# A hybrid decoder layer on one core: shift sums, load order, solve pace and short attention steps

## The chip, the cores and the metric

The kernel runs on one core of a Trainium2 chip. The core has a matrix engine (TensorE, PE in the profile, with its weight loads shown as PEld), a vector engine (VectorE, DVE), a scalar engine (ScalarE, ACT), a general engine (GpSimd, POOL) and a sync engine (SyncE, SP) that here issues nearly all DMA transfers. Each engine works off its own list of instructions in order; semaphores tie the lists together. The metric is the device time of one execution in microseconds (us), less is better.

## The reference

One decoder layer over 512 tokens of width 2048, in float32. Cut to its lines:

```python
mod = silu(c) @ w_ada + b_ada                       # c: [1, 2048], w_ada: [2048, 6144]
shift, scale, gate = split(mod, 3)
h = rms_norm(x, norm_w) * (1 + scale) + shift       # [512, 2048]
aq, ak, av, ag, d_qkv, dz, db, da, mg_a, mg_b = split(h @ w_in)
y_a = (window_attention(rope(norm(aq)), rope(norm(ak)), av, sinks) * silu(ag)) @ w_o_swa
q, k, v = split(silu(causal_conv(d_qkv)))           # 16 + 16 + 32 heads of 128
o = gated_delta_rule(norm(q), norm(k), v, g(da), beta(db))   # chunks of 64, a triangular inverse in each
y_b = (rms_norm(o) * silu(dz)) @ w_o_dn             # w_o_dn: [4096, 2048]
y = sigmoid(mg_a) * y_a + sigmoid(mg_b) * y_b
return x + gate * (y @ w_out)
```

`shift` and `scale` are the two thirds of a vector-matrix product with a 2048 x 4096 weight matrix. The triangular inverse in each chunk is `inv(I + L)` with L strictly lower triangular.

## The kernel before

**Tiles.** All data stand with channels on the 128 partitions and the 512 tokens along the free axis. A float32 product is made of three matmuls on rounded halves: weights and inputs are split into a high part (ACT, `whi`, `hh`) and the remaining low part (DVE, `wlo`, `hl`), and `mm3` (L240 to 245) adds hi x hi, hi x lo and lo x hi into one PSUM tile. A `channel_tile` (L247) makes 128 output channels: 16 steps over the input channels (kt), three matmuls each, 48 in all. The input halves stay in `hh` and `hl`.

**Weights.** `plan` writes one list of weight tiles in the order of use. SP loads each into one of two raw buffers (L203); `split_half` (L55, L56) splits it half by half into three pairs of buffers. A raw buffer is free for the next load when both its halves are split, and a half is split when an earlier one has been used up. `weight_tick` carries out the loads and splits that have come due; it stands in every `pump`.

**Order of the work.** The order of instructions on each engine is written out by the program. `pump` (L84) is called after every second kt of a channel tile, eight times a tile. In a pump, three kinds of side work move on:
- live generators (`go`): each says by its `yield n` after how many pumps its next step comes;
- slow generators (`paced`): a step is taken when the entry's pace, summed over pumps, covers the cost that the step names. `solve` is such: s0 and s1 are the two halves of the triangular inverses (L801 and L808 on DVE by turns, 62 pairs each half);
- side generators (`beside`): queues by name, each with a rate of steps per pump.

Steps that are drained run with no matmuls of a channel tile between them.

**Stages.** Times are those of the profile.
1. Startup, 0 to 180 us. x is normalised and transposed into `xnT`. The 32 column blocks of the conditioning product are summed, 16 for `scale`, then 16 for `shift`: each takes a 1 MB load (`load_ada`, L359, six buffers) and one long DVE operation (L422). Those in `FROM_PE` are summed on PE instead (L413), with a copy on ACT (L418) and a second short matmul (L419). The state pass then multiplies the unshifted input (scale only) with the weights of v and b tiles ("st", seven PSUM tiles side by side, 128x896 halves); `NPRE - NST` mb tiles follow, also unshifted, and all of these results are stored with no shift in them. Meanwhile `shifts` goes through the shift sums. Then the second pass makes `hh`/`hl` again with the shift in (`high(kt, True)`, L438 on ACT, L443 on ACT, L447 on DVE) and multiplies the first tiles by them (`ba`, `k0`).
2. Deltanet A, 180 to 564 us. The k tiles of 15 heads, then `fill` tiles (`mixed`, L151: the mb tiles from `NPRE` on and six ma tiles), with the solve s0 paced at 0.82 beside them. From ma tile 2 on its pace is 1.2, s1 follows. At the end, s0 is drained; its result (`A`, `atmp`) is scaled (L821) and stored (`ta_d` L817, `ts_d` L828).
3. Deltanet B, 564 to 1668 us. Two value heads and a query head at a time: their tiles, the convolution (`conv`, L619 to 634), then loads of the solved blocks and of the decay rows `E` (L751), and the chunk recurrence.
4. The od stage (`branch_b`, L1026), 1668 to 2108 us. In each of two halves 16 `o` tiles are loaded (`oraw`) and split (`oh`, `ol`), two ma tiles are made, then 16 tiles of w_o_dn. Two generators stand beside it on the queue "gate": `shift_products` (L1511) makes what the shift adds to the results stored without it, and `gate` (L1541) makes the third part of the conditioning. A shift product loads a weight block (`sw`), multiplies it by the shift on POOL (L1527), sums it on DVE (`sr`, L1532) and sums over partitions by a matmul with ones (`pshift`, L1534).
5. Attention, 2108 to about 2600 us, four groups of eight heads beside their projections; `attend` (L1237) makes four blocks of 128 tokens: scores S, softmax steps, transposes pP, output O.
6. The products with w_o_swa (os), the merge and the output product, to the end.

The lines the change touches: `NPRE` and `FROM_PE` (L33, L37), the shifted branch of `high` (L437), the loads ahead of the state pass (L481), `shifts` (L512), `s0` and its boost (L662, L671), the two rates (L1034), the yields of `attend` (L1268, L1283, L1302) and `shift_products`. Two lines that a reader needs:

```python
fill = iter([("mb", j) for j in range(NPRE, KT)] + [("ma", j) for j in range(NMA)])   # mixed
src = [st tiles 0..6] + [mb weight tiles NST .. NPRE - 1]                              # shift_products
```

Of the kernel before, what the change touches and what calls it, by code (L numbers as in the profile page):

```python
# [7 lines left out]
F32 = mybir.dt.float32  # L8
# [3 lines left out]
ALU = mybir.AluOpType  # L12
# [17 lines left out]
TWO_PI_LO = 3.0199159819567e-07  # L30
MAGIC = float(0x5F3759DF)
NST = 5
NPRE = 8  # L33
STW = (2 + NST) * P
TRW = 2 * VH + P
NMA = 6
FROM_PE = (0, 1)  # L37


class Layer:  # L40
# [304 lines left out]
    def startup(self, st):  # L345
# [9 lines left out]
        def load_ada(n):  # L355
            if n >= 2 * KT:
                return
            wa = s2.tile([P, D], F32, tag="wa", name="wa", bufs=6)
            nc.sync.dma_start(out=wa, in_=a["w_ada_ss"][n // KT, n % KT])  # L359
            loads[n] = wa  # L360
# [74 lines left out]
        def high(kt, shifted):  # L435
            h32 = s2.tile([P, T], F32, tag="h32", name="h32")
            if shifted:  # L437
                nc.scalar.activation(  # L438
                    h32, xnT[:, kt, :], AF.Identity, scale=scale[:, kt : kt + 1], bias=self.shift[:, kt : kt + 1]
                )  # L440
            else:
                nc.scalar.activation(h32, xnT[:, kt, :], AF.Copy, scale=scale[:, kt : kt + 1])
            nc.scalar.copy(out=self.hh[:, kt, :], in_=h32)  # L443
            return h32
# [33 lines left out]
                ada_sum(0)  # L478
                self.split_half()

        for i in range(3, 7):  # L481
            load_ada(i)
        nxt = high(0, False)
        ada_sum(1)
        low(0, nxt)
# [26 lines left out]
        def shifts():  # L512
            for i in range(4, KT):
                ada_sum(KT + i)
                load_ada(KT + i + 6)
                yield 2

        for n in range(KT + 7, KT + 10):
# [118 lines left out]
    def deltanet(self):  # L637
# [9 lines left out]
        with ExitStack() as ps:  # L647
# [4 lines left out]
            with ExitStack() as sa:  # L652
                wk = sa.enter_context(tc.tile_pool(name="dnA", bufs=2, reuse_waits="tile"))
                sol0 = sa.enter_context(tc.tile_pool(name="sol0", bufs=1, reuse_waits="tile"))
                gp = sa.enter_context(tc.tile_pool(name="gates", bufs=1, reuse_waits="tile"))
                self.go(self.gates(gp), 1)
                self.keys_done, self.solve_in = [], {}
                self.keep_order = True
                self.go(self.keys(wk, 0, self.acc_k), 5)
                self.go(self.solve_load(sol0, 0), 1)  # L660
                self.go(self.solve_load(sol1, 1), 1)
                s0 = self.paced(self.solve(sol0, 0, nc.vector), 0.82)  # L662
                s1 = self.paced(self.solve(sol1, 1, nc.vector), 0.0)
                for kind, j in self.mixed():
                    if kind == "k":
                        self.go(self.keys(wk, j, self.channel_tile(f"k{j}")), 0)
                    elif kind == "mb":
                        self.merge_gate("mb", j, self.mb_d)
                    else:
                        self.merge_gate("ma", j, self.ma_d)  # L670
                        if j == 2:  # L671
                            s0[1] = 1.2
                        if s0 not in self.slow:
                            s1[1] = 1.1
                self.drain_live()
                self.drain_slow(s0)
                self.keep_order = False
                s1[1] = 0.6
# [347 lines left out]
    def branch_b(self):  # L1026
        tc, nc, a = self.tc, self.nc, self.a
        with ExitStack() as es:
# [2 lines left out]
            op = es.enter_context(tc.tile_pool(name="bo", bufs=1, reuse_waits="tile"))  # L1031
            wk = es.enter_context(tc.tile_pool(name="bwk", bufs=2, reuse_waits="tile"))
            self.gwk = es.enter_context(tc.tile_pool(name="gwkb", bufs=1, reuse_waits="tile"))
            self.beside(self.shift_products(wk, pg), 0.3, "gate")  # L1034
            self.beside(self.gate(wk, pg), 0.3, "gate")
            oh = op.tile([P, KT, T], F32R, name="oh")
            ol = op.tile([P, KT, T], F32R, name="ol")
            for half in range(2):
# [197 lines left out]

    def attend(self, wk, kd, n, mask, sink, qs, rs, sg, done):  # L1237
        nc = self.nc
        ao = wk.tile([P, 4, T], F32, tag="ao", name="ao", bufs=1)
        for i in range(NTB):  # L1240
            k0 = 0 if i else P
# [5 lines left out]
            for pp in range(2):  # L1247
# [13 lines left out]
                for e, (ps, t) in enumerate(tl):  # L1261
# [3 lines left out]
                    )  # L1265
                    c = 4 * pp + e
                    nc.vector.tensor_reduce(out=mx[:, c : c + 3 : 2], in_=t[:, :, k0:], axis=AX.X, op=ALU.max)
                yield 2  # L1268
            sk = sink[:, 8 * n : 8 * n + 8]
            nc.vector.tensor_tensor(out=mx, in0=mx, in1=r, op=ALU.mult)  # L1270
            nc.vector.tensor_tensor(out=mx, in0=mx, in1=sk, op=ALU.max)
# [6 lines left out]
            for h in range(8):  # L1278
# [1 line left out]
                nc.scalar.activation(  # L1280
                    t, t, AF.Exp, scale=r[:, h : h + 1], bias=mx[:, h : h + 1], accum_out=den[:, h : h + 1]
                )
            yield 4  # L1283
            nc.vector.tensor_tensor(out=den, in0=den, in1=es, op=ALU.add)
            nc.vector.reciprocal(out=den, in_=den)
            for h in range(8):
# [5 lines left out]
            for kb in kbs:  # L1292
                for e in range(2):
# [5 lines left out]
                    else:  # L1299
                        nc.vector.tensor_copy(out=pT, in_=pt)  # L1300
                    pTs[e, kb] = pT
                yield 2  # L1302
            po = self.psO.tile([P, 4, P], F32, tag="O", name="O")
            for p in range(4):
                for kb in kbs:
# [205 lines left out]
    def shift_products(self, wk, pp):  # L1511
# [2 lines left out]
        st = a["w_st"].rearrange("u p (b c) -> p u b c", b=2)  # L1514
        src = [st[:, :, :, i * P : (i + 1) * P] for i in range(2 + NST)] + [a["w_ch"][96 + j] for j in range(NST, NPRE)]
        ps = pp.tile([P, T], F32, tag="g", name="pshift")
        for n, w_d in enumerate(src):
            w = wk.tile([P, D], F32, tag="gw", name="sw", bufs=1)
            if n < 2 + NST:
# [8 lines left out]
                out=wv, in0=wv, in1=self.shift.unsqueeze(2).to_broadcast([P, KT, P]), op=ALU.mult  # L1528
            )
            yield  # L1530
            r = wk.tile([P, P], F32, tag="sr", name="sr", bufs=1)
            nc.vector.tensor_reduce(out=r, in_=w.rearrange("p (k c) -> p c k", c=P), axis=AX.X, op=ALU.add)  # L1532
            yield
            nc.tensor.matmul(ps[:, n : n + 1], lhsT=r, rhs=self.ones[:, 0:1], start=True, stop=True)  # L1534
        self.bias_v = self.const.tile([P, 2], F32, name="bias_v")
        nc.vector.tensor_copy(out=self.bias_v, in_=ps[:, 0:2])
        self.bias_h = self.const.tile([P, NPRE], F32, name="bias_h")
# [111 lines left out]
```

## Time and profile before

| what | value |
|---|---|
| median of 3 executions | 2968.34 us (2967.02 to 2971.19) |
| the profiled execution, its own time | 2969.02 us |
| its span | 2967.2 us |
| granted TensorE clock, mean | 0.987 |
| PE busy | 2881.7 us, 97% of the span |
| DVE busy | 1864.2 us, 63% |
| ACT busy | 1111.4 us, 37% |
| POOL busy | 270.1 us, 9% |
| moved by DMA | 461.6 MB |

The span is the time from the first to the last instruction of the profiled execution. PE's busy share is an average over all stages; its gaps stand at a few places, and the view of waits names for each what ended it. A row of a time order starts with the start time and the duration in us; "x4" joins four instructions; a bracket gives the idle time before it and what ended it. "SPq" is the DMA queue of SP: the row's duration is the issuing, not the transfer.

### The profile page before, as it was taken

The numbers are of one execution on the slowest core, as the hardware profiler recorded it, in microseconds if no ns is written. First come the engines' busy times: TensorE is split into PE (matmuls) and PEld (weight loads), VectorE is DVE, ScalarE is ACT, GpSimd is POOL, SyncE is SP. The second block draws the span as 40 slices with busy tenths as digits, with TensorE's granted clock in tenths as the row PEclk, the third lists the DMA queues.
The fourth block names the chain that finished last, engine by engine and source line by source line (L and its number), as shares of the span: only waits on it lengthen the run. The fifth ranks groups of instructions, "written<-read, shape, count | busy, mean of one in ns | idle before, by whom it ended". The sixth has DMA issues, their size and how long they took to land.

```text
span 2967.2 us, 37825 instructions
## 1 busy us (share of the span) xinstructions
PE 2881.7 (97%) x14372; PEld 2360.7 (80%) x14372; DVE 1864.2 (63%) x2955; ACT 1111.4 (37%) x2149; POOL 270.1 (9%) x214
## 2 busy tenths in 40 slices
PE   8999999799999999999999999999999999999988
PEld 7867788688888888888888778788788878878867
DVE  7866799777776554555544555543656556554697
ACT  5364433333334433333333322321244444432343
POOL 0002122100000000010000021000100000000011
PEclk9999999899999999999999999999999999999999
DMA  9846555633334433433332566864332223265563
GB/s 364 327 140 183 181 171 157 187 122 117 118 110 127 143 125 114 135 114 126 114 120 94 175 198 221 289 232 160 106 105 89 88 86 104 98 233 178 184 194 93
DMA packets 190041, 461.60 MB, mean 156 GB/s; under 512 B 72706, under 2 KB 89602, under 8 KB 153762
## 3 DMA queue, kind: packets, MB, share of 16 engines
q1 hardware_dynamic: 189858, 459.19, 46.8%
q8 instruction: 113, 1.85, 0.2%
q14 instruction: 70, 0.57, 0.1%
HBM read 397.44 MB, written 59.45 MB: 154 GB/s over the span
## 4 chain that ended last, share of the span: by engine, by line
PE 79%; DVE 6%; DMA 4%; issue 2%; ACT 1%; POOL 1%; SPq 0%; POOLq 0%; DVEq 0%; ACTq 0%
PE mm L243 23%; PE mm L245 22%; PE mm L244 22%; DVE wlo L56 2%; DMA oraw<-o_d 1%; PE S L1256 1%; PE pv L962 1%; PE po L981 1%; PE O L1307 1%; PE pP L277 1%; PE po L980 1%; PE pd L977 1%; PE pp L952 1%; PE m L244 1%; ACT whi L55 1%
## 5 line engine op out<-in xcount | busy, mean ns | idle before, releaser
L243 PE MATMUL mm<-hh,whi 128*128 128x512 f32 x2752 | 1121.7, 408 | 13.3 <-DVE yq L627 9.1
L245 PE MATMUL mm<-hh,wlo 128*128 128x512 f32 x2752 | 1080.5, 393 | 0.5 <-DVE wlo L56 0.5
L244 PE MATMUL mm<-hl,whi 128*128 128x512 f32 x2752 | 1078.3, 392 | 0.2 <-DVE hl L56 0.2
L56 DVE TENSOR_TENSOR wlo<-raw,whi 128x1024 fp32r<-128x1024 f32 (+2 forms) x452 | 565.7, 1254 | 451.6 <-ACT whi L55 446.8
L55 ACT CAST whi<-raw 128x1024 fp32r<-128x1024 f32 (+2 forms) x452 | 470.5, 1043 | 937.7 <-PE mm L244 869.7
L243 PEld LDWEIGHTS mm<-hh,whi 128*128 128x128 f32 x2752 | 519.8, 189 | 122.2 <-issue 17.6
L245 PEld LDWEIGHTS mm<-hh,wlo 128*128 128x128 f32 x2752 | 518.9, 189 | 113.5 <-DVE wlo L56 1.0
L244 PEld LDWEIGHTS mm<-hl,whi 128*128 128x128 f32 x2752 | 520.1, 189 | 99.2 <-issue 0.8
L244 PE MATMUL mm<-ol,whi 128*128 128x512 f32 x512 | 203.2, 397 | 7.0 <-DVE ol L56 7.0
L243 PE MATMUL mm<-oh,whi 128*128 128x512 f32 x512 | 202.8, 398 | 3.3 <-ACT oh L55 2.4
L245 PE MATMUL mm<-oh,wlo 128*128 128x512 f32 x512 | 202.3, 396 | 0.0
L909 POOL TENSOR_TENSOR qe<-qe,yq 128x512 f32<-128x512 f32 x32 | 48.9, 1545 | 910.9 <-DMA qe<-eg_rows 788.9
L758 POOL TENSOR_TENSOR E<-E,neg_g 128x512 f32<-128x512 f32 x64 | 78.8, 1232 | 505.3 <-DVE rkt L66 203.8
L244 PEld LDWEIGHTS mm<-ol,whi 128*128 128x128 f32 x512 | 97.9, 191 | 30.1 <-DVE ol L56 8.9
L243 PEld LDWEIGHTS mm<-oh,whi 128*128 128x128 f32 x512 | 97.5, 191 | 25.9 <-ACT oh L55 3.2
L245 PEld LDWEIGHTS mm<-oh,wlo 128*128 128x128 f32 x512 | 98.0, 191 | 20.3
L808 DVE TENSOR_TENSOR A<-A,atmp 128x62 f32<-128x62 f32 (+30 forms) x124 | 110.5, 891 | 1.5
L801 DVE TENSOR_TENSOR atmp<-A 128x62 f32<-128x62 f32 (+30 forms) x124 | 109.6, 884 | 1.6
L955 DVE SCALAR_TENSOR_TENSOR r<-pp,neg_eg,vt 128x128 f32<-128x128 f32 x96 | 29.3, 347 | 78.8 <-PE pp L952 77.6
L1280 ACT ACTIVATE sm<-sm,mx,rs 128x256 f32<-128x256 f32 (+1 forms) x128 | 71.7, 561 | 3.3 <-DVE mx L1275 3.3
L627 DVE SCALAR_TENSOR_TENSOR yv<-mm,convh,yv 128x511 f32<-128x511 f32 (+2 forms) x96 | 71.5, 744 | 1.6
L422 DVE SCALAR_TENSOR_TENSOR wa<-wa,silu_cb 128x2048 f32<-128x2048 f32 x30 | 68.4, 2284 | 0.0
(348 smaller groups left out, 3311.5 us busy)
## 6 DMA issues: line engine op xcount, KB each, us to landing
raw<-in_w_ch SPq DMA_DIRECT2D x156, 1024.0 KB
wa<-in_w_ada_ss SPq DMA_DIRECT2D x32, 1024.0 KB
raw<-in_w_od SPq DMA_DIRECT2D x32, 1024.0 KB
E<-g_rows SPq DMA_DIRECT2D x64, 256.0 KB
gw<-in_w_ada_gate SPq DMA_DIRECT2D x16, 1024.0 KB
raw<-in_w_os SPq DMA_DIRECT2D x16, 1024.0 KB
qe<-eg_rows SPq DMA_DIRECT2D x32, 256.0 KB
o_d<-zh SPq DMA_DIRECT2D x32, 256.0 KB
```

Of the source, the lines that this page charges most:

```text
L55: self.nc.scalar.copy(out=hi, in_=src)
L56: self.nc.vector.tensor_tensor(out=lo, in0=src, in1=hi.bitcast(F32), op=ALU.subtract)
L243: nc.tensor.matmul(ps, lhsT=wh, rhs=xh, start=first, stop=False)
L244: nc.tensor.matmul(ps, lhsT=wh, rhs=xl, start=False, stop=False)
L245: self.last_mm = nc.tensor.matmul(ps, lhsT=wl, rhs=xh, start=False, stop=last).ins
L422: nc.vector.scalar_tensor_tensor(out=wa, in0=wa, scalar=1.0, in1=scb, op0=ALU.mult, op1=ALU.mult, accum_out=acc)
L627: nc.vector.scalar_tensor_tensor(out=y[:, s:], in0=ps[:, : T - s], scalar=w[:, j : j + 1], in1=y[:, s:], op0=ALU.mult, op1=ALU.add)
L758: nc.gpsimd.tensor_tensor(out=E, in0=E, in1=ng, op=ALU.add)
L801: eng.tensor_tensor(out=t, in0=A[:, m : m + 1, m + 1 :].to_broadcast([P, m, n]), in1=A[:, :m, m : m + 1].to_broadcast([P, m, n]), op=ALU.mult,
L808: eng.tensor_tensor(out=A[:, :m, m + 1 :], in0=A[:, :m, m + 1 :], in1=t, op=ALU.add)
L909: nc.gpsimd.tensor_tensor(out=qf, in0=qf, in1=q, op=ALU.mult)
L1280: nc.scalar.activation(t, t, AF.Exp, scale=r[:, h : h + 1], bias=mx[:, h : h + 1], accum_out=den[:, h : h + 1])
```

## The change

It has five parts, in the order of the program.
- **Startup.** One mb tile fewer is made ahead of the shift (`NPRE` 7), so it becomes one of deltanet A's fills, which see the shift, and one shift product fewer is needed. The first split and the raw load that it frees are put among the loads of the scale blocks 3 to 6, so that the third raw tile of the state pass is loaded after scale block 4. Four shift sums (23, 25, 27, 29) are made on PE, and the generator goes on at once behind them.
- **Second pass.** The shifted input is made by DVE (multiply by scale, add shift) and no longer by ACT.
- **Solve.** s0 runs at 0.88, its boost begins with ma tile 1.
- **Od stage.** Both side generators run at 0.36 steps a pump. `shift_products` waits seven steps, has two buffers for the sums, and issues the short matmul of a product one product later.
- **Attention.** The last group's `attend` has shorter waits between its steps.

```diff
-NPRE = 8
+NPRE = 7
...
-FROM_PE = (0, 1)
+FROM_PE = (0, 1, 23, 25, 27, 29)
...
         def high(kt, shifted):
             h32 = s2.tile([P, T], F32, tag="h32", name="h32")
             if shifted:
-                nc.scalar.activation(
-                    h32, xnT[:, kt, :], AF.Identity, scale=scale[:, kt : kt + 1], bias=self.shift[:, kt : kt + 1]
+                nc.vector.tensor_scalar(
+                    out=h32, in0=xnT[:, kt, :], scalar1=scale[:, kt : kt + 1], scalar2=self.shift[:, kt : kt + 1],
+                    op0=ALU.mult, op1=ALU.add,
                 )
...
-        for i in range(3, 7):
-            load_ada(i)
+        self.split_half()
+        load_ada(3)
+        load_ada(4)
+        self.weight_tick()
+        load_ada(5)
+        load_ada(6)
...
             for i in range(4, KT):
                 ada_sum(KT + i)
                 load_ada(KT + i + 6)
+                if KT + i in FROM_PE:
+                    continue
                 yield 2
...
-                s0 = self.paced(self.solve(sol0, 0, nc.vector), 0.82)
+                s0 = self.paced(self.solve(sol0, 0, nc.vector), 0.88)
...
-                        if j == 2:
+                        if j == 1:
                             s0[1] = 1.2
...
-            self.beside(self.shift_products(wk, pg), 0.3, "gate")
-            self.beside(self.gate(wk, pg), 0.3, "gate")
+            self.beside(self.shift_products(wk, pg), 0.36, "gate")
+            self.beside(self.gate(wk, pg), 0.36, "gate")
...
     def attend(self, wk, kd, n, mask, sink, qs, rs, sg, done):
         nc = self.nc
+        last = n == 3
...
-                yield 2
+                yield 2 - (last and pp)
...
-            yield 4
+            yield 4 - last
...
-                yield 2
+                yield 2 - (last and kb == kbs[0] < kbs[-1])
...
     def shift_products(self, wk, pp):
+        for _ in range(7):
+            yield
         for n, w_d in enumerate(src):
...
-            r = wk.tile([P, P], F32, tag="sr", name="sr", bufs=1)
+            r = wk.tile([P, P], F32, tag="sr", name="sr", bufs=2)
             nc.vector.tensor_reduce(out=r, in_=w.rearrange("p (k c) -> p c k", c=P), axis=AX.X, op=ALU.add)
             yield
-            nc.tensor.matmul(ps[:, n : n + 1], lhsT=r, rhs=self.ones[:, 0:1], start=True, stop=True)
+            if n:
+                nc.tensor.matmul(ps[:, n - 1 : n], lhsT=last, rhs=self.ones[:, 0:1], start=True, stop=True)
+            last = r
+        yield
+        nc.tensor.matmul(ps[:, n : n + 1], lhsT=last, rhs=self.ones[:, 0:1], start=True, stop=True)
```

## The prediction

> **What bounds the kernel now.** I read the head of the page first, then the waits of TensorE (PE), then a table of busy times by stage, and went to the time order of single engines only where those two showed lost time.
>
> ```profile
> span 2967.2 us, 37825 instructions
> PE 2881.7 (97%) x14372; PEld 2360.7 (80%) x14372; DVE 1864.2 (63%) x2955; ACT 1111.4 (37%) x2149; POOL 270.1 (9%) x214
> ```
>
> PE is busy 97% of the span: only its gaps, and stretches at a low clock, can be won without taking work off it. The profiled execution took 2969.02 us, 0.7 us over the median of 2968.34, so a sum made against it holds for the median too.
>
> The gaps, from PE's waits (engine, line, what it waited for: us in total, times, longest):
>
> ```profile
> PE mm L243 <- DVE yq L627: 9.1, 1, 9.1
> PE mm L244 <- DVE ol L56: 7.0, 4, 4.2
> PE ptq L277 <- DVE yq L634: 6.2, 1, 6.2
> PE v L243 <- ACT whi L55: 5.2, 1, 5.2
> PE pshift L1534 <- DVE sr L1532: 4.3, 3, 2.5
> PE mm L243 <- ACT hh L55: 3.9, 1, 3.9
> PE ba L243 <- ACT hh L443: 3.3, 1, 3.3
> PE S L1256 <- DVE sm L1262: 1.6, 1, 1.6
> ```
>
> And the stages around them (window: length, then busy time and instruction count of PE, PEld, DVE, ACT, POOL, then granted clock, DMA share, GB/s):
>
> ```profile
> 153.00:180.00 27.00, 25.00 (x98) 15.99 (x99) 16.50 (x23) 22.89 (x35) 0.00 (x0) 0.94 0.27 84
> 560.00:600.00 40.00, 24.69 (x116) 19.48 (x115) 27.03 (x38) 12.64 (x23) 10.48 (x10) 0.79 0.66 199
> 1670.00:1740.00 70.00, 57.27 (x223) 44.07 (x222) 41.61 (x30) 19.95 (x30) 19.21 (x5) 0.90 0.65 212
> 2595.00:2640.00 45.00, 39.22 (x209) 30.12 (x208) 24.90 (x47) 18.36 (x37) 0.00 (x0) 0.92 0.52 175
> ```
>
> Each gap is followed by a low clock, seen in the last three rows: (1 - clock) x length is 8.4 us in 560-600, 7.0 in 1670-1740 and 3.6 in 2595-2640, beside 15.3, 12.7 and 5.8 us of PE idle. These three places lose 23.7, 19.7 and 9.4 us. The change touches all three, and the startup.
>
> **Startup, the order of loads.** The sixth to eighth scale loads now stand behind the third raw weight of the state pass on SP, no longer ahead of it.
>
> ```profile
> 21.71 15.84 SPq L359 DMA_DIRECT2D wa<-in_w_ada_ss  x6
> 37.65 0.39 SPq L203 DMA_DIRECT2D raw<-in_w_st  x1
> ...
> 56.53 0.79 PE L243 MATMUL v<-hh,whi 128*128 128x512 f32 x1 [5.18 <-ACT whi L55]
> ...
> 56.00:63.00 7.00, 5.93 (x13) 4.26 (x14) 6.96 (x11) 3.22 (x5) 0.00 (x0) 0.51 0.58 206
> ```
>
> The raw load waits behind six 1 MB loads, is issued at 37.65, and PE stalls 5.18 us on its cast, plus 0.5 on the low half, then runs 7 us at clock 0.51 (3.4 lost). With two loads fewer in front I count this stall gone: -9. Bounds: 0 if the stall goes to the scale sums instead, -9 at most.
>
> **Startup, one tile out and four sums in.** A channel tile is 48 matmuls at the spacing of these two rows (9 starts in 2.04 us, 0.227 each): 10.9 us.
>
> ```profile
> 147.67 0.39 PE L245 MATMUL mm<-hh,wlo 128*128 128x512 f32 x1
> 149.71 0.39 PE L245 MATMUL mm<-hh,wlo 128*128 128x512 f32 x1
> ...
> 25.15 1.08 PE L413 MATMUL ada<-wa,silu_cr 128*32 128x128 f32 x32
> ...
> L422 DVE SCALAR_TENSOR_TENSOR wa<-wa,silu_cb 128x2048 f32<-128x2048 f32 x30 | 68.4, 2284 | 0.0
> ...
> 136.66 0.47 SPq L359 DMA_DIRECT2D wa<-in_w_ada_ss  x1
> ...
> 152.40 2.29 DVE L422 SCALAR_TENSOR_TENSOR wa<-wa,silu_cb 128x2048 f32<-128x2048 f32 x1
> ```
>
> The eighth mb tile leaves the startup and becomes a fifteenth fill in the stage of deltanet A: -10.9 and +10.9 on PE. Four sums leave DVE (4 x 2.28 = 9.1 us) for PE (the row's 1.08 each and a short second matmul, 1.15, so 4.6 us). Before, PE went from tile to tile until 149.9 (three tiles back from it, the state pass ended at 117; now at 108) and then waited 3.3 us, because the last of 32 loads was issued at 136.66 and its sum began at 152.40. So the time from the state pass to the shifted pass (117 to the start of the ba matmuls at 149.9 + 3.3, 36 us) was nearly filled by three tiles, 32.7 us. Now it holds two tiles and four sums, 26.4 us, and the loads set its end. In the new order the copies of PE's sums stand on ACT ahead of the copies of the first mb results; the stores of those results, and behind them on SP the last six loads, are held back with them. Working the order through with the durations above I get the last load issued some 28 us after the state pass (before 20) and the shifted pass begun some 39.5 after it, with 13 us of PE idle. That is 108 + 39.5 = 147.5 instead of 153.2, a gain of 6. Bounds: the loads come as early as PE is ready (26.4 us, 13 better), or 8 later still.
>
> **The shifted pass.**
>
> ```profile
> L438 ACT ACTIVATE h<-xnT,shift,scale 128x512 f32<-128x512 f32 x15 | 11.7, 810 | 2.7 <-DVE hl L447 2.7
> ...
> L443 ACT CAST hh<-h 128x512 fp32r<-128x512 f32 x16 | 9.2, 613 | 0.1
> ...
> L447 DVE TENSOR_TENSOR hl<-h,hh 128x512 fp32r<-128x512 f32 x16 | 10.5, 688 | 8.0 <-ACT hh L443 7.9
> ...
> L1082 DVE TENSOR_SCALAR turns<-ang x4: 417/427/428, 2099.3 to 2106.9; 128x512 f32<-128x512 f32 x4
> ```
>
> ACT takes 0.81 + 0.61 = 1.42 us for each of 16 steps, PE 6 matmuls, 1.36. Moving the first to DVE costs there about 0.43 (nearest row, L1082), so 1.12 on DVE against 0.61 on ACT: PE becomes the bound, some 1 us won, but its first steps wait for the late shift values. I book 0. Startup and its moved tile together: -6 + 10.9 = +5, range -8 to +14.
>
> **From deltanet A to B.** The solve is paced at 0.88 in place of 0.82, is boosted from tile ma 1 in place of ma 2, and has one more tile beside it.
>
> ```profile
> 562.35 4.63 DVE L821 TENSOR_TENSOR A<-A,bet 128x1024 f32<-128x1024 f32 x4 [0.66 <-ACT atmp L813]
> ...
> 564.74 5.17 SPq L828 DMA_DIRECT2D ts_d<-A  x4
> ...
> 578.59 0.63 ACT L903 ACTIVATE E<-E 128x512 f32<-128x512 f32 x1 [12.53 <-POOL E L759]
> ```
>
> A queue stands behind the solve's end: DVE scales A, SP stores it (5.17 us), only then loads E, POOL works on E, ACT's exponential of E waits 12.53 us, and the tanh of q is behind it. PE's 9.1 and 6.2 us waits are the two ends of that. In the new order the scaling and its stores stand about two half tiles (10.9 us) earlier against the first q tile, and the tanh stands ahead of the exponential. What stays is the convolution of q and v, interleaved on DVE: I estimate 4.4 us of wait and 1.7 of clock, 6 of 23.7. Gain 18, bounds 5 (all of it merely shifts) and 22.
>
> The cost is DVE's load while the solve runs.
>
> ```profile
> sum 205.00, PE 203.39 PEld 168.07 DVE 189.15 ACT 77.63 POOL 35.49; mean PE 40.68 PEld 33.61 DVE 37.83 ACT 15.53 POOL 7.10
> ...
> L808 DVE TENSOR_TENSOR A<-A,atmp 128x62 f32<-128x62 f32 (+30 forms) x62 | 56.7, 914 | 0.9
> L801 DVE TENSOR_TENSOR atmp<-A 128x62 f32<-128x62 f32 (+30 forms) x62 | 56.3, 909 | 1.0
> ```
>
> From 340 to 545 DVE is busy 189.15 of 205 us, 92%, 113 of them the solve. A pace 7% higher makes it 96%. PE there is at 203.39, so its cover is thin: behind a late low half of a weight all of PE waits. +1, bounds 0 and +10.
>
> **The od stage.** The shift products begin seven steps later, nine in place of ten, with a second buffer for their sums and the matmul of each sum one product late.
>
> ```profile
> 1674.77 4.30 DVE L56 TENSOR_TENSOR wlo<-raw,whi 128x1024 fp32r<-128x1024 f32 x1 [3.01 <-ACT whi L55]
> ...
> 1679.59 3.73 DVE L1532 TENSOR_REDUCE sr<-sw 128x128 f32<-128x2048 f32 x1
> 1683.84 1.22 DVE L56 TENSOR_TENSOR wlo<-raw,whi 128x1024 fp32r<-128x1024 f32 x1
> ...
> 1674.37 3.61 POOL L1527 TENSOR_TENSOR sw<-sw,shift 128x2048 f32<-128x2048 f32 x1 [74.81 <-DMA sw<-in_w_st]
> ```
>
> PE here needs each ol from DVE in time. A product puts two long pieces in its way: the sum (3.73), and one neighbour stretched while POOL multiplies (a low half at 4.30, where 1.22 is usual). Deferring the matmul removes PE's own waits for the sum (4.3, and some 2 of low clock behind them). The later start moves the sums behind more of the ols (behind the 5th, 10th, 13th and 16th, before the 3rd, 7th, 11th and 15th). I take -9, bounds -2 and -16; the missing product lies off the path. The higher rate 0.36 also brings the gate's loads nearer to the second half: 0 to +2, in the bounds.
>
> **The last attention group.** Its steps come to 54 pumps of work where they were 65, so its last output product has about 32 matmuls (7.3 us) of other work behind it.
>
> ```profile
> 2623.16 1.78 SPq L1316 DMA_DIRECT2D ao_d<-ao  x4
> 2625.28 2.62 SPq L1155 DMA_DIRECT2D aoraw<-ao_d  x4
> ```
>
> Store and reload with the cast took until PE's 3.9 us wait ended; now they are nearly covered. 9.4 are lost here; against that stand about 1 us in each of three blocks, whose softmax gets less cover. -6, bounds -9 and -2. A low clock stands here even behind the 1.6 us wait for S. The Trainium skill, TensorE: Matmul & The Clock Gate, Part 1, ties the half clock to an idle window of about 3.4 us; by that the three short waits would be followed by none and 1.7 us of what I leave at 560-600 would go too, which would give 2940. The trace shows low clock behind shorter waits, so the sum keeps it.
>
> **Sum.** 2969.0 + 5 - 18 + 1 - 9 - 6 = 2942.
>
> **The rivals.**
> 1. The startup's tail is worse. If the last loads come 8 us later than I worked out, the startup costs +13, and the sum is 2950; with the cold clock behind the longer idle and PE's sums waiting for their own loads, 2955. For it: the loads stand behind stores on SP. Against it: DVE has four sums fewer to do before the last one.
> 2. The solve's tail only shifts: the convolutions and E still end last. Gain 5 in place of 18: 2955. For it: the scaling still waits for ACT's copies and their stores.
> 3. The od waits move and do not go: nine products still stretch a DVE neighbour, and later ols are as needed as earlier ones; gain 0: 2951. The Trainium skill, GPSIMD Engine Reference, 1 Specifications, says that POOL contends with DVE instructions of two SBUF inputs, which supports this; the row at 4.30 us, beside the 1.22 of the same operation nine us later, agrees.
> 4. Slower: DVE saturates in deltanet A. To pass 2975 it must lose 33 us, about 2 us of PE on each of 16 tiles, that is DVE needing 12.9 us for a tile of 10.9. At 96% it is short of that point, and it would have to reach 118%; a late start of single low halves in bursts could do a part. A slip of 10 us in DVE alone gives 2951.
>
> **How the numbers follow.** Forecast 0.52, its own range 2933 to 2949. Startup worse 0.16, solve's tail 0.11, od waits 0.11, slower 0.10. Two of the middle three together give about 2965, no change. The measurement tells 0.2%, 6 us, from nothing. Faster by more needs under 2962.4: forecast, and the single rivals, less a share for pairs, 0.82; within 0.2%: 0.07; slower: 0.11. The range for 8 in 10 goes from 2929 (startup clean, 13 better) to 2963.
>
> **What would show it.** The changed profile should have no wait of v near 56, a shifted pass beginning near 147 with a longer wait of ba or of PE's sums, the waits for yq at 15.3 down to about 4, pshift at most once, hh below 1 us, and DVE about 96% in the solve. Waits for wlo in deltanet A of tens of us, or PE idle over 20 us before the shifted pass, make me wrong.

## The result and the profile after

The changed kernel takes 2980.36 us in the median (2978.80 to 2983.77), the kernel before 2968.34 (2962.02 to 2971.19): ratio 1.0044, 95% interval 1.0030 to 1.0059. It is slower by 12 us where the prediction had it 26 faster. The profiled execution took 2980.36 us, its span is 2978.6. The kernel before was timed again with each batch of the runs below and had medians of 2968.02 to 2969.34, so medians of different batches are compared as they stand.

The head of the page after, and PE's waits (engine, line, what it waited for: us in total, times, longest). Against the kernel before, lines of the code below `high` have moved by 1, those behind the loads of the startup by 5 to 8, those of the shift products by 10 or 11.

```profile
span 2978.6 us, 38106 instructions
PE 2887.3 (97%) x14506; PEld 2362.3 (79%) x14506; DVE 1858.3 (62%) x2962; ACT 1099.8 (37%) x2136; POOL 272.8 (9%) x213
```

```profile
PE ptkT L277 <- ACT k L719: 12.7, 8, 2.7
PE ada L413 <- DMA wa<-in_w_ada_ss: 12.0, 2, 6.0
...
PE mm L245 <- DVE wlo L56: 6.7, 8, 2.0
PE mm L244 <- DVE ol L56: 6.3, 7, 1.5
PE mm L243 <- DVE yq L634: 5.5, 1, 5.5
PE ba L243 <- ACT hh L444: 4.6, 2, 3.6
...
PE mm L243 <- ACT oh L55: 3.8, 4, 1.9
PE pshift L1545 <- DVE sr L1542: 2.3, 1, 2.3
```

Of the waits before, the second one of the solve's end (ptq, 6.2) and hh (3.9) are gone, yq is down from 9.1 to 5.5, v from 5.2 to 1.9. In their place stand two waits of PE for the loads of its own sums (12.0), eight for low halves (before 0.5 in one), and more for the k tiles (12.7, before 8.1). The waits for `ol` in the od stage have stayed (6.3, before 7.0).

Times between points that both time orders have, in us; the last row ends with the last matmul. Over all the runs below, profiled executions of kernels that share a stage differ in it by up to 5 us in the first, fourth and fifth rows and by up to 3 in the others, so the size of a change is sure to that much only. That there is one is plainer: in the first, second, fourth, fifth and sixth rows the kernels with the old stage and those with the new one stay apart in every profile.

| from, to | before | after | change | forecast |
|---|---|---|---|---|
| start, end of the state pass | 117.1 | 112.3 | -4.7 | -9 |
| to the first ba matmul of the shifted pass | 36.4 | 46.5 | +10.2 | +3 |
| to the end of the pass | 26.4 | 26.1 | -0.3 | 0 |
| to the first od product (one tile more) | 1506.6 | 1511.9 | +5.3 | -6 |
| to the first attention score | 482.2 | 487.8 | +5.6 | -9 |
| to the last O product | 453.5 | 447.7 | -5.8 | with the next -6 |
| to the last matmul | 337.7 | 338.4 | +0.7 | |

### The profile page after: what moved, and what is told of

The parts are those of the page before. It is cut to its first block, busy times and chain, and to the rows that moved or that the text cites. A ratio compares the mean times of both kernels' runs of the same rounds, so it can differ in the third digit from the quotient of the medians.

```text
span 2978.6 us, 38106 instructions
## 1 busy us (share of the span) xinstructions
PE 2887.3 (97%) x14506; PEld 2362.3 (79%) x14506; DVE 1858.3 (62%) x2962; ACT 1099.8 (37%) x2136; POOL 272.8 (9%) x213
## 4 chain that ended last, share of the span: by engine, by line
PE 75%; DVE 7%; DMA 5%; issue 2%; ACT 2%; POOL 1%; SPq 0%; POOLq 0%; DVEq 0%; ACTq 0%
PE mm L243 21%; PE mm L245 21%; PE mm L244 21%; DMA oraw<-o_d 2%; DMA gw<-in_w_ada_gate 2%; DVE wlo L56 2%; PE S L1264 1%; PE pv L969 1%; PE po L988 1%; PE O L1315 1%; PE pP L277 1%; PE po L987 1%; PE pd L984 1%; PE pp L959 1%; DVE sr L1542 1%
## 5 line engine op out<-in xcount | busy, mean ns | idle before, releaser
L56 DVE TENSOR_TENSOR wlo<-raw,whi 128x1024 fp32r<-128x1024 f32 (+1 forms) x452 | 559.9, 1242 | 449.8 <-ACT whi L55 445.2
L55 ACT CAST whi<-raw 128x1024 fp32r<-128x1024 f32 (+1 forms) x452 | 470.4, 1043 | 961.0 <-PE mm L244 874.8
L243 PEld LDWEIGHTS mm<-hh,whi 128*128 128x128 f32 x2752 | 519.7, 189 | 114.6 <-issue 14.3
L245 PEld LDWEIGHTS mm<-oh,wlo 128*128 128x128 f32 x512 | 97.7, 191 | 27.2 <-DVE wlo L56 7.1
L422 DVE SCALAR_TENSOR_TENSOR wa<-wa,silu_cb 128x2048 f32<-128x2048 f32 x26 | 59.4, 2284 | 5.9 <-DMA wa<-in_w_ada_ss 5.9
```

The lines of the kernel that those rows point to most:

```text
L55: self.nc.scalar.copy(out=hi, in_=src)
L56: self.nc.vector.tensor_tensor(out=lo, in0=src, in1=hi.bitcast(F32), op=ALU.subtract)
L243: nc.tensor.matmul(ps, lhsT=wh, rhs=xh, start=first, stop=False)
L245: self.last_mm = nc.tensor.matmul(ps, lhsT=wl, rhs=xh, start=False, stop=last).ins
L422: nc.vector.scalar_tensor_tensor(out=wa, in0=wa, scalar=1.0, in1=scb, op0=ALU.mult, op1=ALU.mult, accum_out=acc)
```

## Experiments on the startup

Two theories for the 10 us: PE's own waits for the loads of sums 27 and 29, or loads that are issued late for everyone. The time order of the changed kernel's startup, first PE, then ACT, then SP ("adas" is ACT's copy of a sum made on PE, "raw<-b" that of a result of the state pass):

```profile
124.45 1.08 PE L413 MATMUL ada<-wa,silu_cr 128*32 128x128 f32 x32
...
131.15 1.08 PE L413 MATMUL ada<-wa,silu_cr 128*32 128x128 f32 x32
...
143.41 1.93 PE L413 MATMUL ada<-wa,silu_cr 128*32 128x128 f32 x32 [5.96 <-DMA wa<-in_w_ada_ss]
...
152.35 1.93 PE L413 MATMUL ada<-wa,silu_cr 128*32 128x128 f32 x32 [6.04 <-DMA wa<-in_w_ada_ss]
```

```profile
125.60 0.27 ACT L418 COPY adas<-ada 128x128 f32<-128x128 f32 x1 [6.56 <-PE ada L413]
125.76 0.59 ACT L514 COPY raw<-b 128x512 f32<-128x512 f32 x1
132.30 0.27 ACT L418 COPY adas<-ada 128x128 f32<-128x128 f32 x1 [5.95 <-PE ada L413]
132.46 0.59 ACT L514 COPY raw<-b 128x512 f32<-128x512 f32 x1
```

```profile
126.38 7.02 SPq L515 DMA_DIRECT2D mb_d<-raw  x2
133.51 0.37 SPq L359 DMA_DIRECT2D wa<-in_w_ada_ss  x1
...
143.35 1.80 SPq L359 DMA_DIRECT2D wa<-in_w_ada_ss  x1
```

One can follow a queue through three engines: the first b result, ready at 112, is copied only at 125.76, because ACT's list has the copy of sum 23 ahead of it, and sum 23 stands behind a channel tile on PE. The stores wait for those copies, and SP's weight loads behind the stores. The last load is issued at 143.35, where it was 136.66.

```diff
-FROM_PE = (0, 1, 23, 25, 27, 29)
+FROM_PE = (0, 1)                    # s_none
+FROM_PE = (0, 1, 23, 25)            # s_2325
+FROM_PE = (0, 1, 27, 29)            # s_2729
```

> The changed kernel with the four shift sums back on VectorE (scale sums 0 and 1 alone on PE). Theory H (held loads: the ACT copies of sums 23 and 25 stand ahead of the copies of the mb results, whose stores hold back the last weight loads on SP): the last load is issued about 20 us after the state pass, near 132 instead of 143 to 145, the shifted pass starts near 148 to 150 instead of 158.9, total 2968 to 2971. Theory P (PE's own waits for the loads of sums 27 and 29, 6 us each, and the low clock behind them): the two waits go, shifted pass near 147, total about 2967. A third view, that the tail is set by the sums on VectorE: four more of 2.28 us each would give no gain, shifted pass near 158, total 2980.

> The changed kernel with 23 and 25 on PE, 27 and 29 back on VectorE. Theory H: the copies of 23 and 25 still hold the stores and loads back, so the last load is issued no earlier than 140 and the shifted pass starts at 156 or later; PE's wait only changes its name from the sum to ba; total 2976 to 2980. Theory P: the two waits of 6 us go and so does most of the low clock: shifted pass near 148, total about 2968.

> The changed kernel with 27 and 29 on PE, 23 and 25 back on VectorE. Theory H: the mb stores and the last loads are issued early (last load near 133 to 136), the PE sums find their loads nearly there, shifted pass near 148 to 151, total about 2969. Theory P: PE still waits for the loads of 27 and 29 for 10 us or more together, shifted pass 155 or later, total about 2977.

Measured: s_none 2969.87 us (ratio to before 1.0002, 0.9992 to 1.0011), s_2325 2976.13, s_2729 2972.43, the last two single runs. The last weight load and the first ba matmul, in s_none, then s_2325, then s_2729:

```profile
133.59 0.39 SPq L359 DMA_DIRECT2D wa<-in_w_ada_ss  x1
143.93 0.69 PE L243 MATMUL ba<-hh,whi 128*64 128x512 f32 x1 [12.18 <-ACT hh L444]
```

```profile
142.47 0.58 SPq L359 DMA_DIRECT2D wa<-in_w_ada_ss  x1
156.73 0.69 PE L243 MATMUL ba<-hh,whi 128*64 128x512 f32 x1 [20.33 <-ACT hh L444]
```

```profile
133.55 0.39 SPq L359 DMA_DIRECT2D wa<-in_w_ada_ss  x1
142.45 0.69 PE L243 MATMUL ba<-hh,whi 128*64 128x512 f32 x1
```

This tells the theories apart. Without 27 and 29 on PE (s_2325), its two waits are gone, but the loads are as late as ever and PE waits 20.33 us for the shifted input instead. Without 23 and 25 (s_2729), the last load is issued at 133.55 and the pass begins 16 us earlier than in the changed kernel, though 27 and 29 still stand on PE and still wait for their loads, 6.7 us in two places. The expectation's third view is out as well: s_none has four sums more on VectorE, and its pass begins 15 us earlier. In s_none and s_2729 it began 4 us or more before what theory H expected. The loads held back are the cause; PE's waits for its own sums were a place where the same lateness showed. Taking all four sums off PE gives back 10.5 us of the 12.

In s_none PE idles 12.18 us before the pass, and the missing tile (10.9) has been moved from that idle time into deltanet A, where PE is the bound. So the next one puts it back.

```diff
-NPRE = 7
+NPRE = 8                            # s_none8, with FROM_PE = (0, 1)
```

> The changed kernel with no shift sums on PE (scale sums 0 and 1 alone) and with the eighth mb tile back in the startup (NPRE 8). Theory L (the last weight load, issued some 10 us before the shifted pass, sets its start, and without the tile PE idles 12 us there): the shifted pass starts within 4 us of the 143.9 of the kernel without the sums, the tile is hidden in that idle time, and deltanet A loses its 10.9 us: total 2959 to 2963. Rival: the tile delays the pass by its own length, start near 155, total 2968 to 2972.

Measured: 2967.13 us (0.9993, 0.9983 to 1.0003); its profiled execution, 2959.32, was the fastest of ten. The pass began at 150.3, 6 us later than in s_none, not within 4, but ended at 174.3 against 172.8: 1.5 us for a tile that costs 10.9 elsewhere. In the four other kernels with this startup (their names begin with n8) it ended at 174.5 to 177.5, so 1.5 is the low end. The total misses the expectation by 4 us in the median, and is 2.7 under that of s_none: the tile is mostly hidden in the trace, and the size of the gain is only partly confirmed.

The load order alone, on the kernel before:

```diff
-        for i in range(3, 7):
-            load_ada(i)
+        self.split_half()
+        load_ada(3)
+        load_ada(4)
+        self.weight_tick()
+        load_ada(5)
+        load_ada(6)
```

> The kernel before with the new load order alone. If the stall of v near 56 was time lost for all of the startup: the state pass ends 5 to 9 us earlier and the total is 2960 to 2964. If the last weight load sets the end of the startup: the state pass ends earlier, PE waits that much longer before the shifted pass, and the total is 2966 to 2970.

Measured: 2965.33 us against 2968.09 (0.9995, 0.9986 to 1.0005): no difference that can be told. The total stands between the two expectations, nearer the second. The state pass ended at 113.8, 3.3 us earlier, the last load was issued at 136.30, where it was 136.66, and PE's wait before the shifted pass grew from 3.3 to 6.2 us. In the trace the second theory holds: what the state pass won, PE mostly waited off again.

The pass with the shift made on ScalarE again:

```diff
-                nc.vector.tensor_scalar(out=h32, ..., op0=ALU.mult, op1=ALU.add)
+                nc.scalar.activation(h32, xnT[:, kt, :], AF.Identity, scale=..., bias=...)
```

> The changed kernel with the shifted input made on ScalarE again. The pass took 26.1 us with VectorE and 26.4 in the kernel before. If ScalarE was its bound, it takes 27 to 29 here with the low clock of the tail, total 2980 to 2983; if the low clock and the order of the first steps set it, 25.5 to 26.5 and no change of the total.

Measured: 2980.36 us in a single run, as the changed kernel. The pass took 27.2 us, 26.1 with VectorE. One microsecond, hidden in the spread of the total: the pass began 2.4 us sooner after the state pass than in the changed kernel (44.1, not 46.5).

## Experiments on the solve

```diff
-                s0 = self.paced(self.solve(sol0, 0, nc.vector), 0.88)
+                s0 = self.paced(self.solve(sol0, 0, nc.vector), 0.82)
...
-                        if j == 1:
+                        if j == 2:
```

on the changed kernel (a_pace, fifteen fills), and on s_none8 (n8_pace, fourteen fills as before).

> The changed kernel with the solve back at pace 0.82 and its boost from ma tile 2. Theory D (the denser solve on VectorE is what makes PE wait in deltanet A, 23.8 us of PE lost between 185 and 570 where the kernel before lost 17.3): that loss falls by 5 to 7 us and the one more tile still ends the solve early enough, so total 2973 to 2976. Theory N (those waits come from where the steps of the key tiles fall in VectorE's order, not from the pace): they change by less than 3 us in sum and the solve ends later, total 2979 to 2988.

> The kernel with no shift sums on PE and the eighth mb tile in the startup, now with the solve at 0.82 and its boost from ma tile 2: the same fourteen fills as the kernel before. From the end of the shifted pass to the first od product the kernel before took 1506.6 us and the one with 0.88 here 1500.6. Theory D (the denser solve costs waits in deltanet A, but with only fourteen fills it ends the solve in time and saves the long wait for yq): 1505 to 1508 here, the wait for yq back at 9 us or more, total 3 to 7 us above the run with 0.88. Rival (the gain of that kernel is a chance of its one profile): 1499 to 1503 and no difference.

Measured: a_pace 2975.97 us (1.0024, 1.0014 to 1.0033), 4.4 below the changed kernel; n8_pace 2970.48 (1.0011, 1.0002 to 1.0020), 3.4 above s_none8; in either pair the intervals just touch. The same edit, back to the lower pace, helps with fifteen fills and costs with fourteen. The waits of PE in a_pace, then n8_pace, then s_none8:

```profile
PE ptkT L277 <- ACT k L719: 9.3, 7, 2.6
PE mm L243 <- DVE yq L634: 5.5, 1, 5.5
```

```profile
PE mm L243 <- DVE yq L634: 9.0, 1, 9.0
PE ptkT L277 <- ACT k L719: 8.8, 7, 2.5
PE ptq L277 <- DVE yq L641: 5.9, 1, 5.9
```

```profile
PE ptkT L277 <- ACT k L719: 11.6, 8, 2.7
PE mm L243 <- DVE yq L634: 3.6, 1, 3.6
```

All profiles with the same fills and pace together:

| fills, pace | waits of the k tiles | waits at the solve's end | end of the pass to the first ptq |
|---|---|---|---|
| 14, 0.82 (before, b_load, n8_pace) | 8.1 to 8.8 | 14.1 to 15.3 | 400.5 to 405.0 |
| 14, 0.88 (s_none8, n8_od, n8_rate, n8_fast) | 11.1 to 12.3 | 3.6 | 398.5 to 401.3 |
| 15, 0.82 (a_pace) | 9.3 | 5.7 | 405.4 |
| 15, 0.88 (changed and seven more) | 10.9 to 13.5 | 5.5 to 6.2 | 409.1 to 413.6 |

The denser solve costs about 3 us in the waits of the k tiles in either case. What it saves at the end, 11 us of waits, is there only while the solve ends too late; the time to the first ptq shows less of it, and its ranges overlap. The fifteenth fill gives the solve the same time by itself; with it the higher pace saves nothing that can be told at the end, and its cost is left. Theory D holds in the waits and in the totals.

## Experiments on the od stage

`o_all` sets the whole stage back, `o_rate` only the two rates.

```diff
-            self.beside(self.shift_products(wk, pg), 0.36, "gate")
-            self.beside(self.gate(wk, pg), 0.36, "gate")
+            self.beside(self.shift_products(wk, pg), 0.3, "gate")
+            self.beside(self.gate(wk, pg), 0.3, "gate")
...
-        for _ in range(7):                                                # o_all only, from here
-            yield
...
-            r = wk.tile([P, P], F32, tag="sr", name="sr", bufs=2)
+            r = wk.tile([P, P], F32, tag="sr", name="sr", bufs=1)
...
-            if n:
-                nc.tensor.matmul(ps[:, n - 1 : n], lhsT=last, rhs=self.ones[:, 0:1], start=True, stop=True)
-            last = r
-        yield
-        nc.tensor.matmul(ps[:, n : n + 1], lhsT=last, rhs=self.ones[:, 0:1], start=True, stop=True)
+            nc.tensor.matmul(ps[:, n : n + 1], lhsT=r, rhs=self.ones[:, 0:1], start=True, stop=True)
```

> The changed kernel with the od stage as before (rates 0.3, no seven steps of delay, one buffer for the sums, the short matmul at once). From the first od product to the first attention score the kernel before took 482.2 us, the changed one 487.8. Theory C (the denser side work on the VectorE and SP lists makes low halves and o tiles late in both halves): 481 to 484, total 2974 to 2977. Rival (the loss comes from the longer stages before it, by a chance position): it stays at 486 to 489, total 2979 to 2982.

> The changed kernel with the two side rates back at 0.3, but with the seven steps of delay, two buffers and the late short matmul kept. Theory R (at 0.36 the sum of a shift product comes 3.8 us a step after its load was issued and not 4.5, while load and multiplication take the same, so VectorE stands idle in front of it, 24.1 us in 4 waits where the kernel before had 15.5, and the low halves queued behind are late): that idle falls to 18 or less, PE's waits for low halves in the od stage from 6.2 to 3 or less, total 2975 to 2978. Rival Q (the delayed start sets where they fall): waits for low halves stay at 5 or more, total 2979 to 2982.

Measured: o_all 2977.94 us (1.0028, 1.0017 to 1.0039), o_rate 2974.79 (1.0019, 1.0010 to 1.0029); the changed kernel had 2980.36 (1.0044, 1.0030 to 1.0059). Setting the rates back alone is worth 5.6 us, setting everything back 2.4, where the intervals overlap. From the first od product to the first score o_all took 484.9 and its total is 2977.94, both a bit over its theory's 481 to 484 and 2974 to 2977 and short of the rival's 486 and 2979. In o_rate VectorE's idle time in front of the sums fell from 24.1 to 18.9 (18 expected), PE's waits for low halves there from 6.2 to 2.7. One way in which the rate does it shows at 1750 to 1770 of the changed kernel (SP, DVE, PE):

```profile
1751.23 0.43 SPq L1532 DMA_DIRECT2D sw<-in_w_st  x1
```

```profile
1764.99 3.79 DVE L1542 TENSOR_REDUCE sr<-sw 128x128 f32<-128x2048 f32 x1 [11.63 <-POOL sw L1537]
1768.71 3.48 DVE L56 TENSOR_TENSOR wlo<-raw,whi 128x1024 fp32r<-128x1024 f32 x3
...
1769.97 0.50 PE L245 MATMUL mm<-oh,wlo 128*128 128x512 f32 x1 [1.96 <-DVE wlo L56]
```

The last part of the load is issued at 1751.23, POOL has multiplied at 1765, and DVE, which took up the sum too early, idles 11.63 us in front of it. Three low halves are queued behind it; ACT had cast the high halves of two of them by 1760 and 1763, so they could have been made in that time, and PE waits for the first. A higher rate doesn't make the loads shorter; it only makes DVE come earlier and wait.

A second way stands further on, beside the gate's sums, whose rate was raised as well:

```profile
1883.69 2.35 DVE L1567 SCALAR_TENSOR_TENSOR gate_bc<-gw,silu_c,gate_bc 128x2048 f32<-128x2048 f32 x1 [4.27 <-DMA gw<-in_w_ada_gate]
...
1887.24 0.51 PE L245 MATMUL mm<-oh,wlo 128*128 128x512 f32 x1 [1.24 <-DVE wlo L56]
```

VectorE waits for a load of the gate, and the low half that PE needs is made behind that sum. PE also waits there for `oh`, whose raw o tiles land late. What the rate does to each of these loads was not tested.

The base without sums on PE (s_none8) tells the three edits of the stage apart: n8_od has the stage as before, n8_rate the delay, second buffer and late matmul at rate 0.3, n8_fast the rate of 0.36 alone.

> The kernel with no shift sums on PE and the eighth mb tile in the startup, solve at 0.88, od stage as in the kernel before. It keeps the load order, the pass on VectorE, the pace and the short attention steps. If the parts add up as the traces have them (startup -5, deltanet A and B -6, attention -7, od 0 to -2 against the changed od stage): 2948 to 2958 in a profile, 2957 to 2965 in the median. If the od stage makes no difference, it stands within 2 us of the same kernel with the changed od stage.

> No shift sums on PE, eighth mb tile in the startup, solve at 0.88, load order, pass and attention steps of the changed kernel, and from its od stage the seven steps of delay, the second buffer and the late short matmul, at the old rate of 0.3. Theory R (the rate alone costs, the late matmul takes away PE's waits for the sums): waits of pshift at most 2.5 us in one place where the kernel with the old od stage has 8.6 in three, total 2955 to 2960. Rival (delay and late matmul only move the waits to the o tiles): from the first od product to the first score 2 us or more over the old od stage's 479.8, total 2961 to 2964.

> The same kernel with the old order of the od stage (no delay, one buffer, short matmul at once) and the new rate of 0.36. Theory R: VectorE's idle time in front of the sums and PE's waits for low halves grow, PE's waits in the od stage are 4 us or more over those at 0.3, total 2964 to 2969. Rival (the rate costs only with the delayed start): within 2 us of the 2960.7 at 0.3.

| kernel | rate | delay, late matmul | median, us | ratio to before (95%) | first od product to first score |
|---|---|---|---|---|---|
| n8_od | 0.3 | no | 2960.65 | 0.9972 (0.9961 to 0.9983) | 479.8 |
| n8_rate | 0.3 | yes | 2956.33 | 0.9956 (0.9942 to 0.9971) | 481.5 |
| n8_fast | 0.36 | no | 2980.57 | 1.0037 (1.0025 to 1.0048) | 494.9 |
| s_none8 | 0.36 | yes | 2967.13 | 0.9993 (0.9983 to 1.0003) | 487.4 |

n8_od came out as its parts add up (2957 to 2965 expected), n8_rate within theory R's total, with a pshift wait of 2.7 where 2.5 was its limit.

The rate alone costs 20 us in n8_fast, at least twice what was expected, 15 of them in the last column and 3 just ahead of it (from the last output of deltanet B to the first od product it took 28.2 us, n8_od 24.8, n8_rate 20.8). PE's waits in n8_fast, and under them VectorE's idle time ahead of the sums, which is 15.4 us in n8_od:

```profile
PE pshift L1542 <- DVE sr L1540: 11.5, 7, 4.0
PE mm L245 <- DVE wlo L56: 6.8, 5, 1.9
```

```profile
  POOL sw L1535: 36.4, 6
```

And PE's waits in n8_rate:

```profile
PE mm L244 <- DVE ol L56: 3.6, 3, 2.3
PE mm L245 <- DVE wlo L56: 3.5, 2, 2.7
...
PE pshift L1545 <- DVE sr L1542: 2.7, 1, 2.7
```

With the short matmul issued at once, each early sum stops PE too (7 times, 11.5 us); issued a product later, it stops it once. So the late matmul and the delay save 13 us at the rate of 0.36, and at 0.3 some 3 to 4 (n8_rate against n8_od, o_rate against o_all; the intervals overlap in both pairs). From the first od product on n8_rate is not shorter than n8_od (481.5 against 479.8): what it saves lies ahead of that point, where the stage begins, 4 us in the profiles. The two edits were not separated from each other.

Three pairs differ in the rates alone. PE's idle time in them, from the last output of deltanet B to the end of the last shift sum, and from there to the end of the last gate sum, in us:

| pair (0.36, 0.3) | beside the shift sums | beside the gate's sums | gain of 0.3 in the median |
|---|---|---|---|
| changed, o_rate | 11.5, 10.2 | 7.1, 3.5 | 5.6 |
| s_none8, n8_rate | 9.5, 10.6 | 9.0, 1.0 | 10.8 |
| n8_fast, n8_od | 14.7, 11.6 | 10.3, 3.1 | 19.9 |

In all three the greater part of the idle time that the higher rate adds stands beside the gate's sums, not beside the shift sums. In n8_fast a lower clock comes on top: from 1658 to 1806, beside the shift sums, the granted clock is 0.92, in n8_od from 1657 to 1811 it is 0.94. What makes up the rest of the 19.9 us stays open.

n8_rate beats both kernels: 11.7 us under before. It is the changed kernel without its sums on PE, with the tile in the startup and the old rates.

## Experiment on the attention steps

```diff
-        last = n == 3
+        last = False
```

> The changed kernel with the last attention group's steps as before. If the shorter steps are what gained between the first attention score and the last output product (before 453.5 us, changed 447.7) and the wait for the reloaded output: 453 to 456 and a wait of hh of 3 to 4 us again, total 2985 to 2989. Rival: the gain there was the low clock and stalls that shifted elsewhere, total 2979 to 2982.

Measured: 2986.88 us (1.0058, 1.0043 to 1.0073), 6.5 above the changed kernel, and 455.7 us from the first score to the last O product (447.7). Two waits are back that the changed kernel doesn't have, while its own wait for pP (2.2 us) is nearly gone:

```profile
PE mm L243 <- ACT hh L55: 4.0, 1, 4.0
PE S L1264 <- DVE sm L1270: 2.0, 1, 2.0
```

## Why the prediction was wrong

**Sums on PE: the step that failed first.** The prediction saw the held stores and loads, and put the shifted pass 39.5 us after the state pass, within bounds of 26 to 47. It was 46.5, at the far end. Rival 1, the tail worse, is what happened in kind. Of the 7 us, 3 lie ahead of the last load's issue, which the step put 28 us after the state pass (it was 31), and 4 between that issue and the pass, which it put 11.5 us apart (it was 15.5; in s_2325, without PE's late sums, 14.3). Rival 1 also held that four sums fewer on VectorE speak against a late tail, while the runs show a tail that moves with the last load (issued at 142.5 to 143.4, pass at 157 to 159; at 133.6, pass at 142 to 144). Behind two waits of 6 us the clock also stayed low into the pass, with PE busy 11.94 of 27 us, so that about half of that, 6 us, was lost to it:

```profile
140.00:167.00 27.00, 11.94 (x83) 7.58 (x84) 15.81 (x25) 6.07 (x11) 0.00 (x0) 0.50 0.73 284
```

**State pass.** The stall was counted as gone, -9; -4.7 in the profile, and alone on the kernel before 3.3 earlier with no measurable gain in the total. Of the stall's waits of 5.2 and 0.5 us, 1.9 and 1.0 were left. And the prediction let 6 of the 9 us through to the start of the shifted pass; in b_load that start hardly moved (153.0, before 153.4).

**The moved tile.** "-10.9 and +10.9 on PE" is right as work, and the sum itself booked a startup only 6 shorter against it. So the move was a loss by the prediction's own numbers; s_none8 and its like show how much of one, with the tile costing 1.5 to 4.7 us in the startup and 10.9 of PE's time as a fill.

**The solve: a gain taken from too large a loss.** The forecast was a gain of 18 and a cost of 1. The wait that is left, 5.5, is near the 4.4 that the step left. But the 23.7 of loss that it started from was too large by the way it was worked out: low clock was multiplied by the whole window and added to the idle time within it. Of the low 17 us, PE was busy in 5.65:

```profile
568.00:585.00 17.00, 5.65 (x15) 4.22 (x16) 9.62 (x15) 3.77 (x12) 5.88 (x6) 0.51 0.72 214
```

so about 2.8 us were lost to the clock beside the 15.3 of idle time, not 8.4. After the change 5.5 of idle time are left, and about 2.2 of clock (from 590 to 600 it is 0.66, with PE busy 6.41 us). That is 18.1 before and 7.7 after, a gain of 10 where 18 stood; the cost in the k tiles was 3 to 5, within the bounds of 0 to 10, but not at 1. With the moved tile, 10.9 - 10 + 4.6 is near the +5.3 of the table. The prediction also took pace, boost and tile as one gain; a_pace shows that the fifteenth fill brings nearly all of it with the old pace. The same error is a small one in the 19.7 of the od stage.

**Od stage.** Forecast -9; in the totals the three edits together cost about 2 (o_all), within the noise of that pair. The place of the waits was read rightly, and rival 3 named the outcome, moved waits, but not the reason. The deferral of the matmul did what was said: pshift waits once, and at a rate of 0.3 it is worth 3 to 4 together with the delay. What the later start was to win at the ols did not come: 7.0 before, 6.3 after. "The higher rate 0.36 also brings the gate's loads nearer to the second half: 0 to +2, in the bounds" is the sentence that failed: the rate costs 5.6 here. It named one place rightly, since 3.6 of PE's idle time that the rate adds stand beside the gate's sums; VectorE's waits for POOL, with low halves behind them, it did not name at all.

**Attention.** -6, and 6.5 measured by t_att; the new waits of pP came to 2.2 in one place, where 3 in all were allowed for.

No low clock followed that wait. In the changed kernel's window around it (length, busy times by engine, granted clock last but two):

```profile
2595.00:2640.00 45.00, 42.69 (x252) 33.73 (x251) 28.00 (x56) 25.49 (x55) 0.00 (x0) 1.00 0.51 168
```

Before, the clock fell here behind a wait of 1.6 us. The Trainium skill, TensorE: Matmul & The Clock Gate, Part 1, has a whole idle window of about 3.4 us as the condition. The wait of 2.2 us agrees with it, the earlier one of 1.6 does not, so a single short wait decides nothing either way; the small term that the sum kept for this is neither confirmed nor refuted.

**Shifted pass.** 0, and nothing measurable; VectorE's operation took 0.54 us, where 0.43 was taken from another line.

The slower rival, VectorE too full in deltanet A, was a part alone. VectorE was as full as forecast (from 350 to 510 it is busy 152.66 of 160 us, 95%), but PE's waits for low halves of weights came to 0.5 us between 185 and 560, and setting the pace back gives 4.4 us, against 10.5 for the sums on PE and 5.6 for the od rates. On the other side the attention steps won 6.5.

## What to carry to other kernels

Work moved to another engine brings its evictions along: look at what stands behind the copy on the engine that makes it, and behind that engine's stores on the DMA queue. Raise the rate of side work only where its loads come in time: here VectorE, which takes its list in order, came early, waited, and held up the low halves behind. Two edits that hide the same wait save it once; test each with and without the other.

## What the runs showed that was not expected

- An increase of the side work's rate from 0.30 to 0.36 steps a pump cost 20 us in one kernel (n8_fast against n8_od), 10.8 in a second (s_none8 against n8_rate) and 5.6 in a third (the changed one against o_rate), though it adds no instruction.
- PE's clock stayed at half for 27 us (140 to 167 in the changed kernel) while PE was busy 44% of the time, with its longest waits at 6 us; the sum of 2.5 us that PE made between the two long waits did not bring it back.
- A tile of 10.9 us of matmuls delayed the end of the startup by 1.5 us where PE had been waiting for late loads (s_none8 against s_none), and by up to 4.7 in the other kernels with that startup.
